# A two-layer hybrid attention and mixture-of-experts block: the sums of squares go behind the first sparse-query projection, the broadcast of their factors into the third

## The chip, the cores and the metric

The kernel runs on one core of a Trainium2 chip. The metric is the device time of one execution in microseconds (us), the median of several runs. The engines are TensorE (PE in the rows; its weight loads are PEld), VectorE (DVE), ScalarE (ACT), GpSimd (POOL) and SyncE (SP), whose queue issues nearly all DMA transfers. Each engine takes its instructions in the order in which the built program holds them.

## What is computed

512 tokens of width 1024 go through two layers. Each layer projects the tokens to many small groups of columns, runs two kinds of attention (a latent one with rotary keys and a sparse one that keeps 128 keys of each query), adds and normalises, and runs 16 experts, two per token. The part that matters here is this:

```python
proj = h @ w_in
qa, kva, kr, dq, dk, dv, iq, ik, iw = jnp.split(proj, SPLIT_POINTS, axis=-1)
# latent group (mla_group)
q = (rms_norm(qa, q_norm_g) @ w_q_up)      # qa has 384 columns
c_kv = rms_norm(kva, kv_norm_g)            # kva has 256 columns
k_nope, v = c_kv @ w_uk, c_kv @ w_uv
# rms_norm(x, g) = x * rsqrt(mean(x * x) + 1e-6) * g
# sparse group (dsa_group): queries dq (512 columns), keys dk, values dv;
# top_k over an index score made of iq, ik, iw selects the keys
```

## The kernel before

Everything is transposed: a projection's output has 128 columns of `w_in` on the partitions and the 512 tokens along the free axis. One such tile is made by `proj(ct)` (line 242): it splits 1024 columns of raw weights into a high and a low part (`granule`, line 170: ACT casts in line 163, and for tiles from the fourth on POOL subtracts in line 164) and multiplies, in `project` (line 266), high weights by high inputs, low weights by high inputs and high weights by low inputs, 8 matmuls each. So a projected tile costs 24 matmuls of 128x512 (line 271), of which the first 8 do without the low weights. The output lies in one of four PSUM buffers `mm`; two more are called `pv`.

The order of the tiles in a layer: S, two `iq`, `dkv`, then two `kva` among the index scores (lines 342 to 373), three `qa`, four `dq`. `qa` tiles are evacuated to `qg` by ACT (line 387) and DVE (line 388), and squared by ACT (line 389) into `sqq`; the third square lies in `sq2`, the second half of the tile `dkv` (the trace calls it dkv). The squares of `kva` are added into `sqk` (line 381). `dq` tiles are evacuated by ACT (line 405) and DVE (line 406) to a tile `dq`, one of nine buffers called `u4`, and copied to their places by DMA.

The norms' factors take this way. Sixteen matmuls with a column of ones (line 418) sum the squares over the partitions, into `pv`: four for `kva`, twelve for `qa`. DVE scales the sums (line 422, `ms`), POOL takes the power -0.5 (line 185, `rmsy`) and multiplies the identity by the factors (line 427, two instructions, the tile `dg`, called `dgt` in the code). Two matmuls of ones by `dg` (line 434) spread the factors over all partitions, one for the keys' side, one for the queries'. With the first, DVE scales `kvg` (line 439), ACT and POOL split it (`big<-kvg`), and PE makes the values v from it and the split weights `wv` (lines 220 to 223, four tiles `vs`). With the second, ACT and DVE make `ct` (lines 443, 444), by which DVE scales the latent queries (line 530, tile `q`). Then the heads begin: scores on PE (line 545), a minimum with the mask on DVE (line 490), exponential on ACT (line 492), scaling on DVE (line 498), transposes on PE (line 502).

All the while DVE has another job: the selection of 128 keys of each query, 16 rounds of MAX and MATCH_REPLACE (lines 365, 366) for each of three token blocks. A round's MATCH_REPLACE needs the MAX's result and the next MAX needs the MATCH_REPLACE's. These rounds have a lower priority (`LOWER`), so the scheduler fills DVE's queue with them between its other work.

A scheduler orders the instructions of each engine at build time, by priority (the order of the code) and by its own estimate of when an operand is there. `tc.issue_after(x)` makes what its block traces on the engine of `x` stand behind `x` there. Before the change the sums are written behind the second `dq` projection and the broadcast behind the third, with no such edge.

Of the kernel before, what the change touches and what calls it, by code (L numbers as in the profile page):

```python
# [17 lines left out]
L, T, D = 2, 512, 1024  # L18
NT = T // 128
# [18 lines left out]
T_S, T_IQ, T_DKV, T_KVA, T_QA, T_DQ = 0, 1, 3, 4, 6, 9  # L38
# [57 lines left out]
def block_kernel(ctx, tc, xT0, x0, win, wqk, wuv, wo, gvec, lnp, rw, rb, wgu, wdn, consts, angles, stripd, rowsd, out):  # L96
    nc = tc.nc
# [19 lines left out]
    def C(name, a=0, b=None):  # L117
        o, w = _C[name]
        return cn[:, o + a:o + (w if b is None else b)]
# [33 lines left out]
    def ps(tag):  # L153
        return psp.tile([128, 512], F32, name=tag, bufs={"mm": 4, "tr": 2, "pv": 2}[tag])
# [76 lines left out]
    def attention(l, xh, xl, wraw, first, rest, x_dram):  # L231
# [5 lines left out]
                    load_win(l, i, wraw)  # L237
            return wraw[s]

        done = {}  # L240

        def proj(ct):
            if l and ct == 0:

                raw((3 + AHEAD) // 2)
                for c in range(4):
                    done[c] = ps("mm" if c > 1 else "tr")
                for a in range(2):
                    if a:
                        rest()  # L250
                    for c in (0, 2):
                        order = (0, 1, 2) if a else (0, 2, 1)
                        for j in order:
                            for d in (c, c + 1):
                                project(done[d], first[d], slice(256 * a, 256 * (a + 1)), (j,), order[2])
            if ct not in done:
                done[ct] = ps("mm")
                project(done[ct], weights(ct), slice(0, T))
            return done.pop(ct)

        def weights(ct, eng=None):
            w = granule(raw(ct // 2), ct % 2, eng or (nc.gpsimd if ct >= 3 else None))
            if ct + AHEAD < N_COLT:
                raw((ct + AHEAD) // 2)
            return w

        def project(p, w, ts, jj=(0, 1, 2), end=2):
            for j in jj:
                for k in range(8):
                    x = (xl if j == 2 else xh)[k // 4][:, k % 4, ts]  # L270
                    nc.tensor.matmul(p[:, ts], w[j == 1][:, k * 128:(k + 1) * 128], x, start=(j + k == 0),  # L271
                                     stop=(j == end and k == 7))

        ke, ko = x4p("ke")
        at = u4("at")
# [10 lines left out]
        p = proj(T_S)  # L286
# [9 lines left out]
        for i in range(2):  # L296
            p = proj(T_IQ + i)
# [8 lines left out]
        p = proj(T_DKV)  # L306
# [7 lines left out]
        p = ps("mm")  # L314
# [6 lines left out]
        p = transpose4(dkv, 0)  # L321
        nc.scalar.copy(dvt, p.rearrange("p (a b) -> p a b", a=NT)[:, :, 64:128])
        p = transpose4(S, 0)
# [7 lines left out]
        sqk = u4p("sqk")  # L331
# [7 lines left out]
        for i in range(1, NT):  # L339
# [3 lines left out]
            for h in range(8):  # L343
                if (i, h) in KVA_AT:
                    latents(KVA_AT.index((i, h)))
                p = ps("mm")
                nc.tensor.matmul(p[:, :n], iq[h // 4][:, h % 4, (i - 1) * 128:i * 128], ik4[:, :n],
                                 start=True, stop=True)
# [4 lines left out]
                w = iwt[:, i, h:h + 1]  # L353
# [16 lines left out]
            for dd in DD[i]:  # L370
                w = dd.shape[1]
# [11 lines left out]
        sqq = list(u4p("sqq")) + [sq2]  # L383
        for i in range(3):
            p = proj(T_QA + i)
# [8 lines left out]
        for i in range(2):  # L394
            w = bigt()
# [4 lines left out]
        dqs = [bigt(F32R).rearrange("p (a b) -> p a b", a=4) for _ in range(2)]  # L400
        vs = bigt().rearrange("p (a b) -> p a b", a=4)
        for i in range(4):
            p = proj(T_DQ + i)
            qh, ql = u4p("dq", F32R)
            nc.scalar.activation(qh, p, AF.Copy, scale=-0.125)
            nc.vector.scalar_tensor_tensor(ql, p, -0.125, qh.bitcast(F32), op0=OP.mult, op1=OP.subtract)
            for s in range(2):
                d = dqs[i // 2][:, i % 2 * 2 + s, :]
                for j, q in enumerate((qh, ql)):
                    b = 64 * (s ^ j)  # L410
                    copy_rows(d[b:b + 64], q[64 * s:64 * (s + 1)])
            if i == 1:

                p = ps("pv")
                for j, qq in enumerate((sqk[:1], sqq)):
                    for t in range(NT):
                        for q in qq:
                            nc.tensor.matmul(p[:, j * 4 + t:j * 4 + t + 1], q[:, t * 128:(t + 1) * 128],
                                             C("ones", 0, 1), start=(q is qq[0]), stop=(q is qq[-1]))
                ms = sm.tile([128, 8], F32, name="ms")  # L420
                for j, n in enumerate((256, 384)):
                    nc.vector.tensor_scalar(ms[:, 4 * j:4 * j + 4], p[:, 4 * j:4 * j + 4], 1.0 / n, 1e-6,
                                            op0=OP.mult, op1=OP.add)
                rs, _ = rsqrt(ms, 8, "rms")
                dgt = u4("dg")
                for j in range(2):
                    nc.gpsimd.tensor_tensor(dgt[:, j * 512:(j + 1) * 512].rearrange("p (t a) -> p t a", t=NT),
                                            ident[:, None, :].to_broadcast([128, NT, 128]),
                                            rs[:, 4 * j:4 * j + 4][:, :, None].to_broadcast([128, NT, 128]), op=OP.mult)
            if i == 2:  # L430
                bc = []
                for j in range(2):
                    p = ps("pv")
                    nc.tensor.matmul(p, C("ones"), dgt[:, j * 512:(j + 1) * 512], start=True, stop=True)
                    bc.append(p)
        ckt = bigt(F32R)
        ckv = [(ckt[:, 1024 * i:1024 * i + 512], ckt[:, 1024 * i + 512:1024 * (i + 1)]) for i in range(2)]
        for i in range(2):
# [13 lines left out]
        for t in range(NT):  # L452
            p = ps("mm")
# [1033 lines left out]
```

## Time and profile before

| | us |
|---|---|
| median of 3 runs (lowest, highest) | 1191.95 (1191.82, 1192.46) |
| the profiled execution | 1192.57 |
| its span, first to last instruction | 1190.8 |
| PE busy with matmuls in the span | 1142.6 (96%) |
| DVE busy | 1020.2 (86%) |
| PE's weight loads busy | 893.5 (75%) |
| ACT busy | 791.2 (66%) |
| POOL busy | 285.6 (24%) |

The mean granted clock of TensorE is 0.986 of full speed. The first layer's attention lies at about 30 to 215 us of the span, the second layer's at about 620 to 805 us. Times in the rows are from the span's start. "128*128 128x512" is a matmul of a 128x128 stationary operand by 512 columns. A row of the timeline can merge several instructions (x24); its second number then runs from the first one's start to the last one's end. Text in brackets at a row's end is the idle time of the engine just before it and what ended that. A float32 matmul that is not marked for the faster format shows as two records, so the two broadcast matmuls are x4, and each sum is x2.

### The profile page before, as it was taken

What the parts mean: (1) busy time and instruction counts of PE and PEld (TensorE: products, weight loads), DVE (VectorE), ACT (ScalarE), POOL (GpSimd) and SP (SyncE); (2) the same over time, 40 slices, a digit from 0 to 9 for tenths busy, and PEclk for the clock granted to TensorE, in tenths of its full rate; (3) what the DMA queues carried; (4) which work ended last, traced back from release to release, by engine and by line L of the source; (5) the groups of instructions that cost most, each with busy time, mean ns of one, the idle gap of its engine ahead of it and who ended that gap; (6) DMA issues with size and microseconds to landing.
All of it is one profiled execution on the core that took longest, in us unless ns stands there. A gap on an engine that the chain in (4) does not pass through costs nothing. (4 is left out here: it accounts for less than half of the span.)

```text
span 1190.8 us, 16760 instructions
## 1 busy us (share of the span) xinstructions
PE 1142.6 (96%) x5705; PEld 893.5 (75%) x5705; DVE 1020.2 (86%) x1858; ACT 791.2 (66%) x1253; POOL 285.6 (24%) x236
## 2 busy tenths in 40 slices
PE   8999899999999999999998998999999999999996
PEld 6786555788788888887696765567887888888873
DVE  4599968399999999988957999774999999999898
ACT  4633668445888888887445346683468888888882
POOL 2345233121111111111132453422212111112011
PEclk9999999999999999999998999999999999999998
DMA  7626104366999999994735170144669999999841
GB/s 263 183 82 203 71 1 142 142 236 247 405 395 393 393 386 375 383 333 176 289 104 151 58 260 2 39 138 155 242 270 397 400 391 389 392 378 375 328 189 71
DMA packets 57547, 292.50 MB, mean 246 GB/s; under 512 B 10309, under 2 KB 14149, under 8 KB 29040
## 3 DMA queue, kind: packets, MB, share of 16 engines
q1 hardware_dynamic: 47664, 270.48, 60.9%
q0 software_dynamic: 8352, 15.66, 3.5%
q10 hardware_dynamic: 1440, 5.24, 1.1%
q8 instruction: 46, 0.75, 0.2%
q14 instruction: 45, 0.37, 0.1%
HBM read 267.96 MB, written 33.03 MB: 253 GB/s over the span
## 5 line engine op out<-in xcount | busy, mean ns | idle before, releaser
L163 ACT CAST hl<-big 128x1024 fp32r<-128x1024 f32 x438 | 457.4, 1054 | 123.0 <-PE mm L1065 51.3
L164 DVE TENSOR_TENSOR hl<-big,hl 128x1024 fp32r<-128x1024 f32 x403 | 483.7, 1227 | 47.7 <-ACT hl L163 41.7
L1064 PE MATMUL mm<-hl,xh 128*128 128x512 f32 x504 | 207.2, 411 | 0.6 <-ACT hl L163 0.6
L1065 PE MATMUL mm<-hl,xh 128*128 128x512 f32 x504 | 197.3, 392 | 0.0
L1086 PE MATMUL pv<-hl,hT 128*128 128x512 f32 x720 | 169.9, 390 | 0.1
L1086 PEld LDWEIGHTS pv<-hl,hT 128*128 128x128 f32 x720 | 134.7, 188 | 28.7 <-DVE hl L164 1.0
L271 PE MATMUL mm<-big,hl 128*128 128x512 f32 (+1 forms) x624 | 140.3, 384 | 2.4 <-ACT big L163 1.7
L271 PEld LDWEIGHTS mm<-big,hl 128*128 128x128 f32 x624 | 112.9, 193 | 27.7 <-ACT hl L163 2.3
L164 POOL TENSOR_TENSOR hl<-big,hl 128x1024 fp32r<-128x1024 f32 x35 | 86.5, 2476 | 133.7 <-ACT hl L163 118.2
L1028 POOL DMA_INDIRECT xg<-xdr,ii x30 | 54.0, 1800 | 268.9 <-DVE ii L1042 242.4
L1064 PEld LDWEIGHTS mm<-hl,xh 128*128 128x128 f32 x504 | 94.8, 188 | 16.8 <-ACT hl L163 1.1
L1065 PEld LDWEIGHTS mm<-hl,xh 128*128 128x128 f32 x504 | 95.1, 189 | 15.7
L1065 PE MATMUL mm<-hl,xl 128*128 128x512 f32 x252 | 98.9, 392 | 0.0
L1064 PE MATMUL mm<-hl,xl 128*128 128x512 f32 x252 | 98.8, 392 | 0.0
L635 PE MATMUL mm<-hl,big 128*128 128x512 f32 x384 | 93.4, 396 | 0.0
L492 ACT ACTIVATE P<-P,mn 128x128 f32<-128x128 f32 (+3 forms) x128 | 71.9, 569 | 17.2 <-DVE mn L490 14.8
L635 PEld LDWEIGHTS mm<-hl,big 128*128 128x128 f32 x384 | 70.8, 188 | 13.6
L1106 POOL DMA_INDIRECT ydr<-y,ii x28 | 30.2, 1079 | 189.4 <-ACT y L1102 117.5
L504 ACT COPY big<-tr 128x512 f32<-128x512 f32 (+3 forms) x128 | 49.8, 432 | 36.5 <-PE tr L502 35.6
L502 PE MATMUL tr<-cn,P 128*128 128x128 f32 x320 | 61.9, 293 | 9.1 <-DVE P L498 8.3
L502 PEld LDWEIGHTS tr<-cn,P 128*128 128x128 f32 x320 | 36.2, 141 | 41.7 <-ACT big L504 17.1
L572 POOL TENSOR_TENSOR mh<-dd,cn 128x256 f32<-128x256 f32 (+2 forms) x64 | 44.6, 718 | 64.9 <-DVE mn L490 39.5
(277 smaller groups left out, 1816.7 us busy)
## 6 DMA issues: line engine op xcount, KB each, us to landing
big<-wgu SPq DMA_DIRECT2D x128, 1024.0 KB, 8.2
big<-wdn SPq DMA_DIRECT2D x64, 1024.0 KB, 7.9
big<-win SPq DMA_DIRECT2D x10, 1024.0 KB, 5.4
ydr<-zz SPq DMA_DIRECT2D x2, 4096.0 KB
big<-wo SPq DMA_DIRECT2D x8, 1024.0 KB, 14.8
big<-ydr SPq DMA_DIRECT2D x8, 1024.0 KB, 12.7
big<-wqk SPq DMA_DIRECT2D x4, 1024.0 KB, 5.1
big<-dq SPq DMA_DIRECT2D x32, 128.0 KB, 2.3
```

Of the source, the lines that this page charges most:

```text
L163: i = nc.scalar.copy(hi, src).ins
L164: last_lo[0] = (eng or nc.vector).tensor_sub(lo, src, hi.bitcast(F32)).ins
L271: nc.tensor.matmul(p[:, ts], w[j == 1][:, k * 128:(k + 1) * 128], x, start=(j + k == 0), stop=(j == end and k == 7))
L492: nc.scalar.activation(e, e, AF.Exp, bias=mn[:, i:i + 1], scale=-1.0, accum_out=su[:, i:i + 1])
L502: nc.tensor.transpose(p[:, (i - kb) * 128:(i - kb + 1) * 128], P[:, PO[i] + kb * 128:PO[i] + (kb + 1) * 128], ident)
L504: copies.append(nc.scalar.copy(pt[kb], p[:, :512 - 128 * kb]).ins)
L572: last_mask[0] = nc.gpsimd.tensor_tensor(m[:, c:c + w], dd, C("slope", h, h + 1).to_broadcast([128, w]), op=OP.mult)
L635: R["pe"] = nc.tensor.matmul(pp[t][i], x, w[:, i * 512:(i + 1) * 512], start=first, stop=last).ins
L1028: return nc.gpsimd.indirect_dma_start(out=st[e]["xg"], out_offset=None, in_=xdr[l], in_offset=bass.IndirectOffsetOnAxis(ap=st[e]["ii"][:, ...
L1064: nc.tensor.matmul(pg, x, w[:, :512], start=(k == 0 and x is a and w is wh), stop=last)
L1065: nc.tensor.matmul(pu, x, w[:, 512:], start=(k == 0 and x is a and w is wh), stop=last)
L1086: nc.tensor.matmul(py[i], x, w[:, i * 512:(i + 1) * 512], start=(k == 0 and x is a and w is wh), stop=last)
```

## The change

Two steps move. The sums of squares and what follows them (`ms`, `rmsy`, `dg`) are written behind the first of the four `dq` projections, not the second, and an edge keeps the sums behind that projection's last matmul on PE. The broadcast is put inside the third `dq` projection: behind its first 8 matmuls (the ones with high weights), ahead of its other 16, with edges on both sides. `project` notes its last matmul for this. No instruction is added or removed in the source.

```diff
-        done = {}
+        done, last_mm = {}, [None]
...
-                    nc.tensor.matmul(p[:, ts], w[j == 1][:, k * 128:(k + 1) * 128], x, start=(j + k == 0),
-                                     stop=(j == end and k == 7))
+                    last_mm[0] = nc.tensor.matmul(p[:, ts], w[j == 1][:, k * 128:(k + 1) * 128], x,
+                                                  start=(j + k == 0), stop=(j == end and k == 7)).ins
...
         for i in range(4):
-            p = proj(T_DQ + i)
+            if i != 2:
+                p = proj(T_DQ + i)
+            else:
+
+                p, w, bc = ps("mm"), weights(T_DQ + i), []
+                project(p, w, slice(0, T), (0,))
+                with tc.issue_after(last_mm[0]):
+                    for j in range(2):
+                        bc.append(ps("pv"))
+                        b = nc.tensor.matmul(bc[j], C("ones"), dgt[:, j * 512:(j + 1) * 512], start=True, stop=True)
+                with tc.issue_after(b.ins):
+                    project(p, w, slice(0, T), (1, 2))
...
-            if i == 1:
+            if i == 0:
 
                 p = ps("pv")
-                for j, qq in enumerate((sqk[:1], sqq)):
-                    for t in range(NT):
-                        for q in qq:
-                            nc.tensor.matmul(p[:, j * 4 + t:j * 4 + t + 1], q[:, t * 128:(t + 1) * 128],
-                                             C("ones", 0, 1), start=(q is qq[0]), stop=(q is qq[-1]))
+                with tc.issue_after(last_mm[0]):
+                    for j, qq in enumerate((sqk[:1], sqq)):
+                        for t in range(NT):
+                            for q in qq:
+                                nc.tensor.matmul(p[:, j * 4 + t:j * 4 + t + 1], q[:, t * 128:(t + 1) * 128],
+                                                 C("ones", 0, 1), start=(q is qq[0]), stop=(q is qq[-1]))
...
-            if i == 2:
-                bc = []
-                for j in range(2):
-                    p = ps("pv")
-                    nc.tensor.matmul(p, C("ones"), dgt[:, j * 512:(j + 1) * 512], start=True, stop=True)
-                    bc.append(p)
```

In the changed kernel the lines of the sums, the broadcast, ACT's and DVE's evacuation of dq, `ms`, `dg` and the scaling of `kvg` are 430, 412, 416, 417, 434, 439 and 445; from there on each line number is 6 higher than before.

The built order moves in the same way in both layers; the excerpts are from the first. On PE, before, from the `qa` and `dq` projections on (120 matmuls are three `qa` and two `dq` tiles):

```order
L271 MATMUL mm<-big,hl 128x512 x120
L418 MATMUL pv<-cn,sqq 128x1 x2
L418 MATMUL pv<-cn,dkv 128x1
L418 MATMUL pv<-cn,sqq 128x1 x2
L418 MATMUL pv<-cn,dkv 128x1
L418 MATMUL pv<-cn,sqq 128x1 x2
L418 MATMUL pv<-cn,dkv 128x1
L418 MATMUL pv<-cn,sqq 128x1 x2
L418 MATMUL pv<-cn,dkv 128x1
L271 MATMUL mm<-big,hl 128x512 x24
L434 MATMUL pv<-dg,cn 128x512 x2
L271 MATMUL mm<-big,hl 128x512 x24
```

On PE, now, the same place (96 matmuls are three `qa` tiles and one `dq` tile; behind the broadcast 40 matmuls follow, 16 of the third and 24 of the fourth `dq` tile):

```order
L271 MATMUL mm<-big,hl 128x512 x96
L430 MATMUL pv<-cn,sqk 128x1 x4
L430 MATMUL pv<-cn,sqq 128x1 x2
L430 MATMUL pv<-cn,dkv 128x1
L430 MATMUL pv<-cn,sqq 128x1 x2
L430 MATMUL pv<-cn,dkv 128x1
L430 MATMUL pv<-cn,sqq 128x1 x2
L430 MATMUL pv<-cn,dkv 128x1
L430 MATMUL pv<-cn,sqq 128x1 x2
L430 MATMUL pv<-cn,dkv 128x1
L271 MATMUL mm<-big,hl 128x512 x32
L412 MATMUL pv<-dg,cn 128x512 x2
```

All sixteen sums now stand behind the first `dq` tile; before, the scheduler had put the four of `sqk` ahead of the `qa` tiles, among the index scores. Between sums and broadcast there are now 32 projection matmuls, where there were 24.

On POOL, before (hl_890 is the low part of the fourth `dq` tile's weights, hl_939 that of `wv`, hl_974 and hl_985 those of the next weights):

```order
L164 TENSOR_TENSOR hl_890<-big_686,hl_890 128x1024
L164 TENSOR_TENSOR hl_939<-wv_746,hl_939 128x1024
L185 TENSOR_TENSOR rmsy_845<-ms_842,mhalf_81 128x8
L427 TENSOR_TENSOR dg_847<-cn_75,rmsy_845 128x512 x2
L164 TENSOR_TENSOR hl_974<-big_748,hl_974 128x1024
L164 TENSOR_TENSOR hl_985<-big_748,hl_985 128x1024
```

On POOL, now:

```order
L164 TENSOR_TENSOR hl_890<-big_686,hl_890 128x1024
L185 TENSOR_TENSOR rmsy_810<-ms_807,mhalf_81 128x8
L439 TENSOR_TENSOR dg_812<-cn_75,rmsy_810 128x512 x2
L164 TENSOR_TENSOR hl_939<-wv_746,hl_939 128x1024
L164 TENSOR_TENSOR hl_974<-big_748,hl_974 128x1024
L164 TENSOR_TENSOR hl_985<-big_748,hl_985 128x1024
```

The power and the two products with the identity have moved ahead of the split of `wv`.

On ACT, before, with the semaphores that each instruction waits for (the first `dq` tile is dq_783; it takes the buffer in which `wv` lay, so it waits for POOL's split of `wv`):

```order
L389 ACTIVATE dkv_299<-mm_715 128x512 [waits DVE_49]
L163 CAST hl_939<-wv_746 128x1024 [waits DMAHW7_49,PE_49,Pool_49]
L405 ACTIVATE dq_783<-mm_755 128x512 [waits Pool_49]
L163 CAST hl_974<-big_748 128x1024 [waits DMAHW5_49,PE_49]
L405 ACTIVATE dq_818<-mm_790 128x512 [waits PE_49]
```

On ACT, now (dq_783 takes the buffer of `sqq`, free when PE has made the sums; it is the second tile, dq_843, that takes the buffer of `wv`):

```order
L389 ACTIVATE dkv_299<-mm_715 128x512 [waits DVE_49]
L416 ACTIVATE dq_783<-mm_755 128x512 [waits PE_49,Activation_49]
L163 CAST hl_939<-wv_746 128x1024 [waits DMAHW7_49,Pool_49]
L416 ACTIVATE dq_843<-mm_815 128x512 [waits PE_49,Pool_49]
L163 CAST hl_974<-big_748 128x1024 [waits DMAHW5_49]
```

The wait for POOL's split of `wv` has passed from the first `dq` tile to the second. On DVE, now, from `ms` on to the second `dq` tile (before, `ms` stood four rounds later and behind the first `dq` tile, and the second `dq` tile one round behind `ms`):

```order
L434 TENSOR_SCALAR ms<-pv 128x4 x2
L366 MATCH_REPLACE aw<-m_493,aw 128x384
L417 SCALAR_TENSOR_TENSOR dq<-mm,dq 128x512
L365 MAX m_496<-aw 128x8
L366 MATCH_REPLACE aw<-m_496,aw 128x384
L365 MAX m_499<-aw 128x8
L366 MATCH_REPLACE aw<-m_499,aw 128x384
L365 MAX m_502<-aw 128x8
L366 MATCH_REPLACE aw<-m_502,aw 128x384
L365 MAX m_505<-aw 128x8
L366 MATCH_REPLACE aw<-m_505,aw 128x384
L417 SCALAR_TENSOR_TENSOR dq<-mm,dq 128x512
```

and DVE, before, the same step:

```order
L406 SCALAR_TENSOR_TENSOR dq<-mm,dq 128x512
L366 MATCH_REPLACE aw<-m_499,aw 128x384
L365 MAX m_502<-aw 128x8
L366 MATCH_REPLACE aw<-m_502,aw 128x384
L365 MAX m_505<-aw 128x8
L422 TENSOR_SCALAR ms<-pv 128x4 x2
L366 MATCH_REPLACE aw<-m_505,aw 128x384
L365 MAX m_508<-aw 128x8
L406 SCALAR_TENSOR_TENSOR dq<-mm,dq 128x512
```

So `ms` stands at the MAX of m_493 now, and between it and the second `dq` tile lie the rest of that round, the first `dq` tile and four whole rounds. From the second `ct` on, DVE's order is as before. SP's order is the same in both kernels.

## Rows read from the trace of the kernel before

**Rows 1.** Busy time by stretch, both layers; columns: engines' busy us, granted clock, DMA.

```profile
core 0: us, PE busy (x) PEld busy (x) DVE busy (x) ACT busy (x) POOL busy (x), PEclk, DMA share, GB/s
43.00:134.00 91.00, 85.98 (x368) 64.93 (x369) 87.75 (x218) 40.99 (x85) 34.97 (x20) 0.96 0.41 138
633.60:724.60 91.00, 85.38 (x368) 64.85 (x368) 87.65 (x217) 40.80 (x84) 32.40 (x19) 0.96 0.39 132
```

**Rows 2.** Timeline of PE, layer 1; columns: start, us, engine, line, operation, operands, idle.

```profile
59.62 24.57 PE L271 MATMUL mm<-big,hl 128*128 128x512 f32 x107
84.03 0.50 PE L418 MATMUL pv<-cn,sqq 128*128 128x1 f32 x4
...
86.63 5.75 PE L271 MATMUL mm<-big,hl 128*128 128x512 f32 x24
94.17 3.00 PE L434 MATMUL pv<-dg,cn 128*128 128x512 f32 x4 [1.80 <-POOL dg L427]
96.19 7.21 PE L271 MATMUL mm<-big,hl 128*128 128x512 f32 x24
103.24 0.39 PE L220 MATMUL mm<-hl,big 128*128 128x512 f32 x1
```

**Rows 3.** Timeline of PE, layer 2.

```profile
684.80 2.12 PE L434 MATMUL pv<-dg,cn 128*128 128x512 f32 x4 [1.79 <-POOL dg L427]
...
692.25 0.39 PE L220 MATMUL mm<-hl,big 128*128 128x512 f32 x1
...
705.98 3.11 PE L545 MATMUL mm<-ke,q 128*128 128x384 f32 x4 [1.00 <-DVE q L530]
```

**Rows 4.** Timeline of DVE, layer 1.

```profile
85.11 0.56 DVE L365 MAX8 m<-aw 128x8 f32<-128x384 f32 x1
...
87.61 0.56 DVE L365 MAX8 m<-aw 128x8 f32<-128x384 f32 x1
88.09 0.67 DVE L406 SCALAR_TENSOR_TENSOR dq<-mm,dq 128x512 fp32r<-128x512 f32 x1
...
89.32 0.56 DVE L365 MAX8 m<-aw 128x8 f32<-128x384 f32 x1
...
91.05 0.21 DVE L422 TENSOR_SCALAR ms<-pv 128x4 f32<-128x4 f32 x2
...
116.59 0.28 DVE L490 CUSTOM_DVE_ANT_0 P<-mm,at 128x128 f32<-128x128 f32 x1
```

**Rows 5.** Timeline of DVE, layer 2: the same first minimum.

```profile
707.23 0.28 DVE L490 CUSTOM_DVE_ANT_0 P<-mm,at 128x128 f32<-128x128 f32 x1
```

**Rows 6.** Timeline of ACT, layer 1.

```profile
80.83 0.60 ACT L389 ACTIVATE dkv<-mm 128x512 f32<-128x512 f32 x1 [0.26 <-DVE qg L388]
...
85.42 0.60 ACT L405 ACTIVATE dq<-mm 128x512 fp32r<-128x512 f32 x1 [3.06 <-POOL hl L164]
```

**Rows 7.** Timeline of POOL, layer 1.

```profile
91.34 1.66 POOL L185 TENSOR_TENSOR rmsy<-ms,mhalf 128x8 f32<-128x8 f32 x1 [5.96 <-DVE ms L422]
...
95.07 4.71 POOL L164 TENSOR_TENSOR hl<-big,hl 128x1024 fp32r<-128x1024 f32 x2
```

**Rows 8.** Busy time in the three stretches in which the granted clock was 0.50.

```profile
95.30:98.70 3.40, 3.40 (x7) 1.98 (x8) 3.26 (x9) 0.00 (x0) 3.40 (x2) 0.50 0.51 119
149.90:153.30 3.40, 3.05 (x10) 2.10 (x12) 3.40 (x15) 1.98 (x7) 1.37 (x3) 0.50 0.00 0
706.30:709.70 3.40, 3.40 (x6) 1.68 (x5) 3.37 (x13) 1.70 (x6) 0.00 (x0) 0.50 1.02 329
```

**Rows 9.** Timeline of DVE later in the heads, layer 1, then the same instructions, layer 2.

```profile
136.22 0.43 DVE L164 TENSOR_TENSOR big<-pv,big 128x256 fp32r<-128x256 f32 x1 [1.45 <-ACT big L163]
...
158.56 0.29 DVE L490 CUSTOM_DVE_ANT_0 P<-mm,at 128x128 f32<-128x128 f32 x1 [2.02 <-PE mm L545]
...
727.35 0.43 DVE L164 TENSOR_TENSOR big<-pv,big 128x256 fp32r<-128x256 f32 x1 [1.57 <-ACT big L163]
...
748.57 0.29 DVE L490 CUSTOM_DVE_ANT_0 P<-mm,at 128x128 f32<-128x128 f32 x1 [1.31 <-PE mm L545]
```

## The prediction, written before the changed kernel ran

> **What bounds the kernel now.** I read the busy time by stretch first. From the start of the index selection to the first softmax DVE is busy 87.75 of 91 us in layer 1 and 87.65 in layer 2, PE with matmuls 85.98 and 85.38 [rows 1]; the rest of DVE's time is the small step between instructions, and the list of waits has no DVE entry in either stretch. So two engines are nearly full, and busy time alone doesn't say which sets the pace.
>
> The timeline of PE shows what the change aims at: PE reaches the broadcast and idles 1.80 us in layer 1 and 1.79 in layer 2 until POOL has `dg` [rows 2, 3]. In layer 1 the granted clock is then 0.50 (the 1.2 GHz level) from 95.3 to 98.7 [rows 8], and the fourth `dq` tile takes 7.21 us, the third 5.75 [rows 2].
>
> Whether that wait costs anything can be read by laying the layers side by side, since only one of them had the slow clock there. The broadcasts start at 94.17 and 684.80, 590.63 apart. The values' first matmul starts at 103.24 and 692.25, 589.01 apart: layer 2's PE has gained 1.62 us [rows 2, 3]. The first minimum on DVE starts at 116.59 and 707.23, 590.64 apart [rows 4, 5]: **the gain is gone to 0.01 us**. A little before it, layer 2's PE stood still for DVE's latent queries, 1.00 us in one place [rows 3]. So in this stretch DVE sets the pace, and time that PE saves ends as a longer wait for DVE.
>
> **The change part by part.** I follow layer 1; layer 2 has the same order and durations. Each step starts from the trace's own time and adds durations.
>
> *The sums.* 107 matmuls take 24.41 us up to the sums (59.62 to 84.03), 0.228 each, a tile 5.47. The first `dq` tile ends one tile ahead of the old sums, at 78.56. Twelve sums take 2.60 us (84.03 to 86.63), 0.217 each; the four of `sqk` that now join them 0.87 [rows 2]. But the third square is not there: ACT makes it from 80.83 to 81.43, because it stands behind DVE's evacuation of the third `qa` tile [rows 6]. PE, whose queue holds the sums ahead of the second `dq` tile, gets through `sqk` and two more sums by about 79.9 and **waits some 1.5 us until 81.43**. Ten sums remain, 2.2 us: they end at 83.7.
>
> *The factors.* DVE takes `ms` at the MAX that starts at 85.11; its slot opens 0.48 later, as `dq`'s does at 87.61, so at 85.59 [rows 4]. The sums are there; no wait. From `ms` to the broadcast's first `dg` the trace has 3.12 us (91.05 to 94.17) [rows 2, 4]; `dg` is there at 88.7, its second half a microsecond on.
>
> *The broadcast.* PE runs the second `dq` tile from 83.7 to 89.2 and 8 matmuls of the third (1.82) to 91.0. `dg` is there: the wait of 1.80 is gone. The broadcast takes 2.02 at most (94.17 to 96.19, partly at the slow clock), then 40 matmuls 9.1: the values start at 102.1. In layer 1 that is 1.1 us earlier than 103.24, in layer 2 0.5 later than 101.62 (692.25 less 590.63). PE has traded one wait for another, and the sums of `sqk`, which stood in a stretch where PE waited for ACT, now stand in its full stretch.
>
> *POOL's queue and what it holds up.* This is the term that I think reaches the end. The power and both products now stand ahead of the split of `wv`. In the trace the split behind them starts 4.02 us behind `ms` (91.05 to 95.07) and takes 2.36 (half of 4.71) [rows 4, 7]. From 85.59 that gives an end at 91.97. The buffer of `wv` is what the second `dq` tile is written to; in the kernel before the first `dq` tile had it, and ACT stood 3.06 us for that same split [rows 6]. So ACT writes the second `dq` tile from 92.0 to 92.6, though PE has had it since 89.2. DVE's part stands behind it in DVE's strict order. DVE gets there at 91.7: from 85.11 one round with a `dq` in it (1.71, as 87.61 to 89.32), three plain rounds (1.25, half of 85.11 to 87.61) to 90.57, and about 1.15 of a fourth [rows 4]. **DVE waits 0.9 us**, and it had no wait in this stretch. What else moves on DVE keeps its count; a `dq` costs 0.46 there whichever gap of a round it fills (1.71 less 1.25), and the scaling of `kvg`, which no longer stands next to a `dq`, fills one gap more, which I estimate at 0.1 gained. Net +0.8 us on DVE per layer.
>
> *What is late next.* POOL splits `kvg` behind the next two weights, and the second of these waits for the third `dq` tile, on PE at 96.7; with ACT's and POOL's steps as in [rows 6, 7] its end comes at about 102.7, when PE wants it. PE's fourth `v` tile waits for a buffer that DVE frees with the last `dq`; PE then comes to the first scores no later than before in layer 1, and at most half a microsecond later in layer 2, where it waited 1.00 for DVE. Neither moves DVE. SP's order is unchanged, and its copies of `dq` move by less than a transfer's slack to the first sparse head.
>
> *Does a DVE delay last to the end?* A delay that the slow clock gave layer 2 at its first scores is still 0.49 at 727.35, against layer 1 (591.13 - 590.64) [rows 4, 5, 9], and up to there DVE has no idle time to give back until the 1.45 us ahead of 136.22, which is the end of a chain that itself starts at DVE.
>
> **Sum.** Two layers by 0.8: +1.6 to +1.7 us. On the profiled execution's 1192.57 that is 1194.2; the runs' median lies 0.62 below that execution, so I expect 1193.6. The unknown is how much of 0.8 arrives. Its bounds: nothing (the later idle on DVE takes it up), 1.8 (two layers by 0.9).
>
> **Rivals.**
>
> *Nothing arrives* (1192.0). The 1.45 us ahead of 136.22 [rows 9] would have to be slack of its own and swallow 0.8. Against it: it ends a chain through DVE's own softmax.
>
> *PE sets the pace after all* (1189). If DVE's rounds could slide, the lost idle time of 1.80 and 1.79, and the slow clock's 1.62, would all count: at most -5.2, of which the new wait of 1.5 per layer takes 3.0 back, so -2.2; with a shorter new wait, because the third square comes earlier, -3. The alignment to 0.01 us speaks against it. The Trainium skill's page "Perfetto Trace Analysis", section "Optimization Strategies", says that the matmul engine should be kept as busy as possible and that what it waits for is to be optimised. By that rule this change takes away the right wait; the rows of DVE say otherwise here, where the two layers show what such a wait was worth.
>
> *Slower by the clock* (1195.0). PE now idles 1.5 us behind the first `dq` tile, and DVE's 0.8 is added to PE's waits at the first scores. In the trace the granted clock was 0.50 three times [rows 8]. Where it hits the projections, DVE doesn't notice. Where it hits the heads, DVE waits for PE: from the minimum of 116.59 to 136.22 the layers part by 0.49 (706.3 to 709.7 was in layer 2), and from 136.22 to 158.56 they come together by 1.12 (591.13 to 590.01), which is layer 1's stretch of 149.9 to 153.3 [rows 4, 5, 8, 9]. One more such stretch in the heads costs 0.5 to 1.1; from the first scores on it counts. With one added, 1193.6 + 1.1 and a little: about 1195. For it: more idle time on PE just ahead of the heads. Against it: the old idle time of 1.80 is gone, and the stretch at 95.3 with it.
>
> *The broadcast still waits*, so that the change doesn't do what it says: `dg` at 88.7 against 91.0 leaves 2.3 us; I give it nothing of its own.
>
> **How the numbers follow.** Forecast 1193.6: 0.52. Nothing arrives, 1192.0: 0.17. PE sets the pace, 1189: 0.10. Slower by the clock, 1195.0: 0.21. A measurement can tell about 0.2%, 2.4 us: below 1189.6 is faster, above 1194.3 slower. Most of the third rival is faster, 0.07; the last one and the upper edge of the forecast (a stall of 0.9 kept whole, and a stretch of slow clock half counted) are slower, 0.27; the same 0.66. The range from 1191.2 to 1195.4 leaves out PE's rival and the last one with two such stretches.
>
> **What would show it.** Right: DVE idle about 0.9 us ahead of its second `dq` (line 417), released by ACT, in both layers; PE idle 1.5 us at the sums (line 430), released by ACT, and none at line 412; DVE's first minimum about 0.8 later from its selection's start than before (116.59), while the values on PE start earlier in layer 1. Wrong: DVE without that idle time, which would mean POOL or the buffer was quicker than I read; or DVE's first minimum earlier than before, which would mean that PE set the pace.

## The result, and the profile after

The changed kernel takes 1199.72 us, the median of five runs (1197.81 to 1200.04). Five runs of the kernel before, beside them, gave 1191.95 us (1190.41 to 1194.26). The ratio is 1.0053, 95% interval 1.0042 to 1.0064: **slower by 6.3 us**, outside the range of 1191.2 to 1195.4. This ratio is not the quotient of the two medians, which is 1.0065 or 7.8 us; the text goes by the ratio throughout. The profiled execution took 1200.04 us, its span 1198.3 (before: 1192.57 and 1190.8).

The timeline of PE in the changed kernel, the place of [rows 2], answers first: the sums (line 430), the second tile and a third of the third (line 271 x32), the broadcast (line 412) and the values' first matmul (line 220). The first four rows are of layer 1, the next three of layer 2.

```profile
81.54 0.38 PE L430 MATMUL pv<-cn,dkv 128*128 128x1 f32 x2 [1.98 <-ACT dkv L389]
...
85.44 9.12 PE L271 MATMUL mm<-big,hl 128*128 128x512 f32 x32
94.40 1.88 PE L412 MATMUL pv<-dg,cn 128*128 128x512 f32 x4
...
105.23 0.39 PE L220 MATMUL mm<-hl,big 128*128 128x512 f32 x1
...
675.58 0.38 PE L430 MATMUL pv<-cn,dkv 128*128 128x1 f32 x2 [1.85 <-ACT dkv L389]
...
679.58 9.01 PE L271 MATMUL mm<-big,hl 128*128 128x512 f32 x32
688.42 1.88 PE L412 MATMUL pv<-dg,cn 128*128 128x512 f32 x4
```

The wait of 1.80 us at the broadcast is gone: line 412 has no bracket. In its place PE waits 1.98 and 1.85 us for the third square. Then 32 matmuls take 9.12 us where 24 took 5.75 before [rows 2]. The reason stands in the busy time by stretch (columns as in [rows 1]; the granted clock is the third figure from the end): half clock, the 1.2 GHz level, for 6.8 us behind the wait, in both layers, and two more stretches in the heads.

```profile
43.00:134.00 91.00, 85.52 (x357) 65.81 (x358) 86.23 (x210) 37.50 (x75) 34.73 (x20) 0.94 0.42 138
...
82.00:88.80 6.80, 6.80 (x26) 6.12 (x26) 6.51 (x19) 1.54 (x2) 3.85 (x4) 0.50 0.18 41
675.90:682.70 6.80, 6.80 (x26) 6.13 (x26) 6.53 (x19) 1.54 (x2) 3.76 (x3) 0.50 0.18 46
153.70:157.10 3.40, 3.40 (x12) 2.02 (x12) 3.40 (x12) 2.64 (x9) 1.36 (x3) 0.50 0.00 0
747.60:751.00 3.40, 3.40 (x12) 2.06 (x14) 3.40 (x14) 2.40 (x9) 1.36 (x3) 0.50 0.00 0
```

DVE is the engine that the prediction followed. Its timeline in layer 1, and the POOL rows of the same microseconds:

```profile
93.47 0.69 DVE L417 SCALAR_TENSOR_TENSOR dq<-mm,dq 128x512 fp32r<-128x512 f32 x1 [1.61 <-ACT dq L416]
...
104.11 1.57 DVE L368 TENSOR_TENSOR aw<-aw 128x384 f32<-128x384 f32 x1
105.60 0.68 DVE L365 MAX8 m<-aw 128x8 f32<-128x512 f32 x1
106.20 1.04 DVE L372 SCALAR_TENSOR_TENSOR dd<-aw,at 128x384 f32<-128x384 f32 x1
```

```profile
89.67 2.41 POOL L164 TENSOR_TENSOR hl<-wv,hl 128x1024 fp32r<-128x1024 f32 x1
...
101.60 2.41 POOL L164 TENSOR_TENSOR hl<-big,hl 128x1024 fp32r<-128x1024 f32 x1 [4.77 <-ACT hl L163]
103.97 2.86 POOL L164 TENSOR_TENSOR big<-kvg,big 128x512 fp32r<-128x512 f32 x2
```

Two losses stand there. DVE waits 1.61 us at its second `dq` (1.51 in layer 2), the place that was predicted, with 0.9. And the last two instructions of the third block's selection, the comparison (line 368) and the distances (line 372), take 1.57 and 1.04 us. Before they took 0.55 and 0.54, and POOL's split of `kvg` was over at 102.3, ahead of them. Now the two meet. The rows before:

```profile
102.45 0.55 DVE L368 TENSOR_TENSOR aw<-aw 128x384 f32<-128x384 f32 x1
...
103.52 0.54 DVE L372 SCALAR_TENSOR_TENSOR dd<-aw,at 128x384 f32<-128x384 f32 x1
```

```profile
99.77 2.55 POOL L164 TENSOR_TENSOR big<-kvg,big 128x512 fp32r<-128x512 f32 x2
102.38 0.95 POOL L448 MEMSET zz<- 128x1024 f32 x1
```

POOL's memset, which reads no tile, ran beside the comparison there and cost it nothing. MAX8 (line 365), which stands between the two in the changed kernel beside the same split, takes its usual 0.68. Layer 2 has the same pair, 1.57 and 1.04 us.

Laid side by side instruction by instruction, DVE is 0.06 us later than before until 85, 1.67 later behind the wait, 3.2 later behind the two long instructions, and stays near there to the end of the layer (3.5); layer 2 adds another 3.1, and its heads 0.9. That makes the 7.5 us by which the two profiled spans differ. Per layer: 1.6 of waiting and 1.5 of collision, (1.57 + 1.04) - (0.55 + 0.54). Twice that is 6.2, beside 6.3 by the ratio.

### The profile page after: what moved, and what is told of

Read it like the earlier page. It is cut to its first block, busy times and chain, and to the rows that moved or that the text cites. A ratio compares the mean times of both kernels' runs of the same rounds, so it can differ in the third digit from the quotient of the medians.

```text
span 1198.3 us, 16756 instructions
## 1 busy us (share of the span) xinstructions
PE 1149.7 (96%) x5705; PEld 898.4 (75%) x5705; DVE 1022.8 (85%) x1858; ACT 790.7 (66%) x1253; POOL 285.5 (24%) x236
```

## Experiments

Each ran beside the kernel before on the same chip; a difference in us is its ratio less one, on about 1193.

### The sums alone

```diff
-            if i != 2:
-                p = proj(T_DQ + i)
-            else:
...
+            p = proj(T_DQ + i)
...
+            if i == 2:
+                bc = []
...
+                    nc.tensor.matmul(p, C("ones"), dgt[:, j * 512:(j + 1) * 512], start=True, stop=True)
```

> Only the sums are moved: they stand behind the first tile of the third projection, as in the changed kernel; the broadcast stands behind the third tile, as in the kernel before. Theory (the loss comes with the sums: PE waits 1.98 us for the third square, works at a granted clock of 0.50 afterwards, so the second tile comes late and DVE waits 1.6 us, and the POOL split of kvg then lies beside DVE's L368 and L372, 1.5 us): all three are still there, the time is that of the changed kernel, 1198.5 to 1200.5. Rival (the broadcast inside the tile is what costs): the time is that of the kernel before, 1191 to 1193.

Measured 1197.07 us, ratio 1.0024 (1.0015 to 1.0034): +2.9 us, between theory and rival. DVE's rows:

```profile
94.17 0.69 DVE L406 SCALAR_TENSOR_TENSOR dq<-mm,dq 128x512 fp32r<-128x512 f32 x1 [1.47 <-ACT dq L405]
...
104.94 0.94 DVE L368 TENSOR_TENSOR aw<-aw 128x384 f32<-128x384 f32 x1
106.41 0.53 DVE L372 SCALAR_TENSOR_TENSOR dd<-aw,at 128x384 f32<-128x384 f32 x1
```

The wait is whole, the collision only touches (0.38 us a layer). So the sums bring the wait; the broadcast's new place moves POOL and DVE against each other by the rest.

### The sums eight matmuls later

Inside the second tile, behind its first eight matmuls, where the third square is there:

```diff
-            if i == 0:
+            elif i == 1:
+                p, w = ps("mm"), weights(T_DQ + i)
+                project(p, w, slice(0, T), (0,))
...
+                with tc.issue_after(bz.ins):
+                    project(p, w, slice(0, T), (1, 2))
```

> The changed kernel with the sums eight matmuls later, inside the second tile, where the third square (ready at 81.4 us in the first layer) is there already. Theory (PE's wait for the square starts the loss): no wait of PE at the sums, granted clock 1.00 through the second tile, no wait of DVE of over 0.3 us at the second tile's remainder, the kvg split on POOL back at about 99 to 102 us and L368 and L372 at 0.55 and 0.54 us; time 1191 to 1193. Rival (what costs is that the factors come early, so that POOL does rms and dg ahead of the split of wv): DVE still waits about 0.9 us, time 1193.5 to 1196. Second rival (the broadcast's two matmuls inside the third tile put PE behind for the heads): 1197 or more with no wait of DVE before 100 us.

Measured 1198.21 us, 1.0037 (1.0027 to 1.0048): +4.4 us. The theory's PE part came true: no wait at the sums and a clock of 1.00 from there to 110 us (PE waits 1.12 us ahead of the eight matmuls instead, and 1.00 at the broadcast). Its time did not. The rows of ACT, DVE and POOL in turn:

```profile
94.85 0.60 ACT L438 ACTIVATE dq<-mm 128x512 fp32r<-128x512 f32 x1 [4.99 <-POOL hl L164]
```

```profile
95.48 0.69 DVE L439 SCALAR_TENSOR_TENSOR dq<-mm,dq 128x512 fp32r<-128x512 f32 x1 [0.91 <-ACT dq L438]
...
104.41 0.55 DVE L368 TENSOR_TENSOR aw<-aw 128x384 f32<-128x384 f32 x1
105.47 2.22 DVE L372 SCALAR_TENSOR_TENSOR dd<-aw,at 128x384 f32<-128x384 f32 x1
```

```profile
92.44 2.38 POOL L164 TENSOR_TENSOR hl<-wv,hl 128x1024 fp32r<-128x1024 f32 x1
...
104.88 2.40 POOL L164 TENSOR_TENSOR hl<-big,hl 128x1024 fp32r<-128x1024 f32 x1
```

With PE out of the way the wait is 0.91 us, released through ACT by POOL's split of `wv`: the prediction's own term, in place and size. And another split of POOL now meets the distances, which take 2.22.

### The second tile in a buffer of its own

```diff
-            qh, ql = u4p("dq", F32R)
+            qh, ql = (h2("dq", F32R), h2("dq", F32R)) if i == 1 else u4p("dq", F32R)
```

> The changed kernel with the second tile of dq in a buffer of its own, so that its copy on ACT no longer needs the buffer that POOL's split of wv frees at 92.08 us; every queue has the same order. Theory (in the changed kernel DVE's wait of 1.6 us is set by PE, whose second tile is ready only at 92.8 us after the stretch at a granted clock of 0.50): the wait stays at 1.5 to 1.7 us in each layer and the time at 1198 to 1200.5. Rival (the step of the prediction: POOL's split of wv sets the wait): the wait falls under 0.3 us and the time to 1196 to 1197.5.

Measured 1196.37 us, 1.0031 (1.0018 to 1.0044): +3.7 us, and the row decides for PE:

```profile
92.79 0.60 ACT L416 ACTIVATE dq<-mm 128x512 fp32r<-128x512 f32 x1 [6.42 <-PE mm L271]
```

```profile
93.42 0.69 DVE L417 SCALAR_TENSOR_TENSOR dq<-mm,dq 128x512 fp32r<-128x512 f32 x1 [1.54 <-ACT dq L416]
...
104.06 0.55 DVE L368 TENSOR_TENSOR aw<-aw 128x384 f32<-128x384 f32 x1
105.13 1.05 DVE L372 SCALAR_TENSOR_TENSOR dd<-aw,at 128x384 f32<-128x384 f32 x1
```

The buffer is free and DVE waits 1.54 us, nearly as long as in the changed kernel (2.71 in layer 2, where the half clock lasted longer, and 0.28 at `ms`). So two causes end within a microsecond of each other, PE's tile at 92.8 and POOL's split at 92.1; taking one away shows the other. In this run the comparison escaped: it starts at 104.06 and goes through, and POOL's `kvg` split of 104.03 takes 3.29 us instead of 2.55. But the longer wait of layer 2 takes most of that back (5.6 against 6.2 in the table below), so why the time is 1.6 us below the expected isn't shown.

### The comparison and the distances later

```diff
+                if i == 3 and k == 3:
+                    with tc.issue_after(mr):
+                        distances(2, *held)
...
+            if i == 2:
+                held = work, acc
+            else:
+                distances(i, work, acc)
```

> The changed kernel with DVE's two instructions of two SBUF operands on the third block (the comparison that ends its selection and the distances, L368 and L372, 1.57 and 1.04 us in the changed kernel) moved behind the fourth round of the fourth block's selection, to about 111 to 113 us of the first layer, past POOL's split of kvg (103.97 to 106.83 us). Nothing else moves in any queue. Theory (they are slow because POOL's split runs beside them): 0.55 and 0.54 us there, or one of the two still longer if the next split of POOL (about 112 us) reaches it; 1.0 to 1.5 us less in each layer, time 1196.5 to 1198. DVE's wait of 1.6 us at the second tile stays. Rival (they are slow by what they wait for, or PE sets the pace there): the same time as the changed kernel, 1199 to 1200.5.

Measured 1196.17 us, 1.0028 (1.0018 to 1.0038): +3.3 us, where the changed kernel has +6.3. As the theory has it:

```profile
111.49 0.54 DVE L374 TENSOR_TENSOR aw<-aw 128x384 f32<-128x384 f32 x1
112.56 0.53 DVE L378 SCALAR_TENSOR_TENSOR dd<-aw,at 128x384 f32<-128x384 f32 x1
```

With the waits of 1.58 and 1.60 us left, 3.2 is what remains, and 3.3 is measured.

### All three taken away

The sums later, the buffer, and the distances behind the third round (`k == 2`), together.

> The changed kernel with all three causes taken away: the sums eight matmuls later (no wait of PE for the third square), the second tile of dq in a buffer of its own (no wait for POOL's split of wv), and DVE's L368 and L372 behind the third round of the fourth block's selection, at about 108 to 111 us, where POOL is idle. Theory (these three are the whole loss, and DVE sets the pace, so that PE's gain is worth nothing): no wait of DVE over 0.3 us between 80 and 112 us, L368 and L372 at 0.55 and 0.54 us, and the time of the kernel before within 1 us, 1192 to 1194. Rival (PE's freed 1.8 us a layer do reach the end once nothing else is lost): 1189 to 1191. Second rival (something else of the change costs time as well): 1195 or more.

Measured 1192.14 us beside 1192.63, 0.9996 (0.9987 to 1.0005): **the loss is gone, and nothing is gained.** DVE's rows show no wait over 0.3 us between 80 and 112 us and 0.56 and 0.54 for the pair. PE's rows at the broadcast and the first scores show what becomes of its lead in layer 1 (1.3 us at 98 us, once DVE's starts ahead of the change are set equal):

```profile
91.36 2.12 PE L445 MATMUL pv<-dg,cn 128*128 128x512 f32 x4 [0.99 <-POOL dg L433]
...
114.60 0.92 PE L565 MATMUL mm<-ke,q 128*128 128x128 f32 x4 [0.67 <-ACT ke L556]
116.22 1.77 PE L565 MATMUL mm<-ke,q 128*128 128x384 f32 x4 [0.70 <-DVE q L550]
122.75 0.33 PE L522 MATMUL tr<-cn,P 128*128 128x128 f32 x1 [1.03 <-DVE P L518]
```

The wait of 0.67 us for ACT stands in the kernel before too. For DVE PE waits 0.70 and 1.03 us, where it waited 0.63 in the kernel before: 1.1 of the 1.3 us end there. The run tests less than its expectation says. PE still waits about 1 us at the broadcast in both layers, and in layer 2 it comes to the values no earlier than before (693.40 and 692.25 us, with DVE's start 1.1 us later in this profile). So only layer 1 gave PE a lead, and the rival, which counted on 1.8 us a layer, was not tried in full.

### POOL beside DVE in the kernel before

```diff
         zz = u4("zz")
+        for i in range(2):
+            nc.gpsimd.tensor_sub(zz[:, 512 * i:512 * (i + 1)], kvg[0], kvg[1])
```

> The kernel before with two idle subtractions of 128x512 on POOL (their result is overwritten by the memset of zz) right behind the split of kvg, so that POOL works beside DVE's L368 (102.45 us) and L372 (103.52 us) as it does in the changed kernel; DVE, PE and ACT have the same order as before. Theory (the collision alone costs 1.5 us a layer, and DVE sets the pace): L368 and L372 take about 1.5 and 1.0 us, time 1194 to 1195.5. Rival (DVE has slack behind this point, or POOL's work does not slow it): 1191.5 to 1192.5.

The rows are as the theory has them, without any other part of the change:

```profile
103.53 1.54 DVE L368 TENSOR_TENSOR aw<-aw 128x384 f32<-128x384 f32 x1
105.60 1.03 DVE L372 SCALAR_TENSOR_TENSOR dd<-aw,at 128x384 f32<-128x384 f32 x1
```

```profile
103.35 2.87 POOL L448 TENSOR_TENSOR zz<-kvg 128x512 f32<-128x512 f32 x2
```

The time is not: 1194.12 us lies in the expected range, but the kernel before took 1193.41 beside it; the ratio is 1.0003 (0.9994 to 1.0012), +0.4 where two collisions of 1.5 make 3.0. In its trace DVE is 1.5 us later behind the pair and 0.65 later at 158 us; of layer 2's 1.5, 1.25 remain. The same with one long subtraction instead of two short ones:

```diff
+        nc.gpsimd.tensor_sub(zz, kvt, kvt)
```

> The kernel before with one idle subtraction of 128x1024 on POOL (about 2.4 us) behind the split of kvg, in place of the two of 128x512 (about 1.3 us each) of the earlier run; the same bytes, and every other queue as in the kernel before. Theory (DVE's instruction with two SBUF operands makes no progress until POOL's running instruction ends): L368, which starts with it at about 102.5 us, takes 2.4 to 2.8 us instead of 1.5, and L372, which then comes behind it, 0.55. Rival (the two share what they need and both go slower): L368 1.0 to 1.6 us and L372 about 1.0 us, as with the two short ones. Time in either case 1193 to 1196.

```profile
103.15 2.13 DVE L369 TENSOR_TENSOR aw<-aw 128x384 f32<-128x384 f32 x1
...
105.81 0.53 DVE L373 SCALAR_TENSOR_TENSOR dd<-aw,at 128x384 f32<-128x384 f32 x1
```

```profile
102.97 1.90 POOL L448 TENSOR_TENSOR zz<-kvg 128x1024 f32<-128x1024 f32 x1
```

One long POOL instruction, one long DVE instruction, and the next one free: DVE's comparison ends 0.41 us behind POOL's end (105.28 and 104.87), a little less than its own 0.55. So the two don't share in this row: DVE stands until POOL's instruction is over. Time 1195.20, 1.0012 (1.0003 to 1.0022), +1.4 for 3.2 on DVE. Where the rest of such a delay goes in the kernel before stays open: its own profile has a stretch of half clock in the heads at 149.9 us [rows 8] that neither of these two profiles has, which may be much of it.

### PE kept busy through its wait

Sixteen small matmuls whose result isn't used stand ahead of the sums (`warm`), and the second tile has a buffer of its own as above:

```diff
-                with tc.issue_after(last_mm[0]):
+                with tc.issue_after(warm(8, p, last_mm[0])):
                     for j, qq in enumerate((sqk[:1], sqq)):
```

> The changed kernel with the second tile of dq in a buffer of its own and 16 small matmuls of 256 columns, whose result is not used, put ahead of the sums, so that PE works through the 2 us in which it waits for the third square. Theory (the idle time at the sums is what the granted clock of 0.50 follows): clock 1.00 through sums and second tile, the sums in 2.5 us or less instead of 3.7, the second tile ready at 89 to 90 us instead of 92.8. Rival (the low clock has another origin): 0.50 there all the same, and the second tile at 92 to 93 us. The queue of DVE has another order here, so the whole time decides nothing.

One execution, 1200.63 us. By stretch:

```profile
78.00:85.00 7.00, 6.57 (x54) 6.10 (x54) 6.72 (x17) 4.31 (x7) 2.36 (x1) 1.00 0.28 77
85.10:88.50 3.40, 3.40 (x9) 2.67 (x8) 3.26 (x11) 0.50 (x1) 0.55 (x1) 0.50 0.17 39
```

Theory and rival are each right in part: the sums behind the wait, 0.43 us now, run at full clock (81.63 to 83.89, 2.3 us against 3.9), but the clock still falls, later and for half as long, and ACT has the second tile at 91.28 (92.84 in the changed kernel). In layer 2, where PE still waited 1.69 us, the clock fell for 6.8 us.

### Less work on DVE, and the changed kernel again

Three runs leave out one round of selection, of the fourth block (the third with `i == 2`):

```diff
-            for _ in range(16):
+            for _ in range(16 - (i == 3)):
```

> The kernel before with 15 rounds of selection instead of 16 for the fourth block (it keeps 120 keys there instead of 128), which takes one MAX8, one load and one MATCH_REPLACE8 of 512 columns, 0.69, 0.09 and 0.68 us, off DVE in each layer and nothing off PE. Theory (DVE sets the pace from the selection to the end of the heads' first part): 1.4 us less in each layer, 1189.5 to 1191.5. Rival (PE sets the pace): no difference, 1192.5 to 1194.

Measured 1193.67 us, 1.0008 (1.0000 to 1.0017): no gain. The round is taken off the end of the fourth block's selection, at about 141 us, and there DVE now waits for PE:

```profile
142.42 0.69 DVE L530 TENSOR_TENSOR q<-mm,ct 128x512 f32<-128x512 f32 x1 [0.78 <-PE mm L223]
144.48 0.69 DVE L530 TENSOR_TENSOR q<-mm,ct 128x512 f32<-128x512 f32 x1 [0.76 <-PE mm L223]
```

That is the rival's outcome: PE holds DVE up as soon as DVE has a round less here, so DVE alone does not set the pace to the end of the selection. How far it does, this run doesn't say.

> The kernel of the run with all three causes taken away, with 15 rounds of selection instead of 16 for the third block (it keeps 120 keys there instead of 128): 0.56, 0.09 and 0.54 us less on DVE in each layer, ahead of the first scores. The queue of DVE is planned anew behind it. Theory (PE comes early to the first scores there and waits for DVE's queries, 0.67 and 0.70 us at 114.6 and 116.2 us, so DVE's time counts in full): 1.2 us less in each layer than without, 1189 to 1191 where the kernel before takes 1192 to 1193.5. Rival (behind the first scores PE sets the pace): 1191.5 to 1193.5.

> The same round less for the third block in the kernel before, 1.2 us less on DVE in each layer. Theory (in the kernel before PE comes to the first scores only 0.67 us ahead of DVE's queries, 114.95 us, so no more than that can be gained): 0 to 0.7 us less in each layer, 1191 to 1193. Rival (DVE alone sets the pace in the kernel before too): 2.4 us less, 1189.5 to 1191.

Both became slower, +4.5 us (1.0038, 1.0025 to 1.0051) and +2.4 us (1.0020, 1.0011 to 1.0029), and decide nothing on the pace. A shorter queue was planned anew, and the new order brought collisions: the comparison took 1.00 and in layer 2 2.58 us, the distances 1.43, in the first; 0.81 and 0.98 in the second.

> The changed kernel again, unaltered, beside the kernel before on one chip, so that it stands on the same footing as the other runs. Theory (two waits of DVE of 1.6 us and two collisions of 1.5 us, 6.2 us in all): 1198 to 1200 where the kernel before takes 1192 to 1193.5. Rival (part of the first difference came from stretches at half clock that only some executions have): 1196.5 to 1198.

Measured 1200.35 us, just above the expected, 1.0059 (1.0046 to 1.0073): +7.0 us, with waits of 1.59 and 1.63 and the same 1.57 and 1.04 in both layers. The sum from DVE's rows is 6.3.

The sums of DVE's waits and of the pair's excess over 0.55 + 0.54, both layers, against the times:

| kernel | waits | pair | sum | measured (95%) |
|---|---|---|---|---|
| changed | 3.1 | 3.0 | 6.2 | 6.3 (5.0 to 7.6) |
| changed, again | 3.2 | 3.0 | 6.3 | 7.0 (5.5 to 8.7) |
| sums later | 1.8 | 3.4 | 5.2 | 4.4 (3.2 to 5.7) |
| own buffer | 4.5 | 1.0 | 5.6 | 3.7 (2.1 to 5.2) |
| sums alone | 3.1 | 0.8 | 3.8 | 2.9 (1.8 to 4.1) |
| distances later | 3.2 | 0.0 | 3.2 | 3.3 (2.1 to 4.5) |
| all three | 0.0 | 0.0 | 0.0 | -0.5 (-1.6 to 0.6) |
| before, two short | 0.0 | 3.0 | 3.0 | 0.4 (-0.7 to 1.4) |
| before, one long | 0.0 | 3.2 | 3.2 | 1.4 (0.4 to 2.6) |

Each sum is of one profiled execution, each time of all of them. Six of the nine sums lie in their intervals; those of the own buffer and of the kernel before with POOL's extra work lie above. One reason shows in the traces. In these three, in the sums alone, the sums later, the distances later and the changed kernel again, DVE's delay shrinks by 1.1 us between 135 and 157 us of layer 1, where the profile of the kernel before has its half clock [rows 8] and theirs have none. How many executions of the kernel before have that stretch isn't known.

## Why the prediction was wrong, step by step

- **That DVE sets the pace, so that PE's wait was worth nothing**: right as far as it was tested. The wait at the broadcast went, and no time came of it; with the three losses taken away the time is that of before, and the lead that PE then had in layer 1 ended as waits for DVE. It does not hold to the end of the selection: with a round less, DVE waits for PE at 142 us.
- **PE waits 1.5 us at the sums**: right in place, 1.98 and 1.85 in size; PE came there earlier than reckoned.
- **The second tile from 83.7 to 89.2**: the first step that failed. The rows that it was made from have full clock. The changed kernel has half clock from 82.0 to 88.8; ten sums took 3.9 us instead of 2.2, and ACT had the tile at 92.84. The prediction said of a half clock in the projections that "DVE doesn't notice"; with the sums in front of the tile it does. So the values on PE, which were to start earlier in layer 1, start at 105.23, 2.0 us later than before [rows 2].
- **POOL holds the second tile, DVE waits 0.9**: the mechanism is there (split of `wv` over at 92.08, predicted 91.97; 0.91 us with PE's lateness gone), but in the changed kernel PE ends later than POOL. So the sign that was named, DVE idle at line 417 and released by ACT, came in the right place with another cause behind it, which is chance. The term is 1.6, not 0.8 a layer: 1.5 of the 4.6 us by which the sum was short.
- **What is late next: the split of `kvg`, "when PE wants it", "neither moves DVE"**: failed, and it is the larger part, 3.0 us. The split's end was put at 102.7; it came at 106.8, and from its start at 103.97 it runs beside DVE's comparison. I asked only who waits for the split, not what runs beside it. The Trainium skill has the rule, on the page "SBUF — State Buffer", section "SBUF: two separate sides": VectorE with two SBUF inputs and a GpSimd instruction that reads SBUF share one pair of ports under an exclusive lock, held for a whole instruction, and the loser blocks. The rows agree (2.13 us beside one long instruction, 1.54 and 1.03 beside two short ones). Such a meeting could have been read from the kernel before, as the rows under this list show.
- **A delay of DVE lasts to the end**: it did here (table, first rows); for a collision alone in the kernel before less than half was measured.
- **Slower by the clock**: the rival's stretches in the heads did come in the profile, two of them, and DVE's delay grows there by 0.3 to 0.9 us; it is not what makes the 6 us.

The kernel before has such meetings of its own. Where DVE adds up the index scores (line 358, two SBUF operands), one instruction takes 0.60 us alone and 2.76 and 2.74 beside POOL's splits, and ends 0.4 us behind each split:

```profile
64.40 2.76 DVE L358 SCALAR_TENSOR_TENSOR aw<-big,iwt,aw 128x384 f32<-128x384 f32 x1
...
67.74 0.60 DVE L358 SCALAR_TENSOR_TENSOR aw<-big,iwt,aw 128x384 f32<-128x384 f32 x1
...
70.13 2.74 DVE L358 SCALAR_TENSOR_TENSOR aw<-big,iwt,aw 128x384 f32<-128x384 f32 x1
```

```profile
64.02 2.72 POOL L164 TENSOR_TENSOR hl<-big,hl 128x1024 fp32r<-128x1024 f32 x1 [2.60 <-ACT hl L163]
69.46 3.00 POOL L164 TENSOR_TENSOR hl<-big,hl 128x1024 fp32r<-128x1024 f32 x1 [2.72 <-ACT hl L163]
```

Layer 2 has 2.75 us twice (655.03 and 660.75). A timeline over the whole stretch merges fourteen of these instructions into one row, and the two long ones don't stand out. So some 4.3 of the 87.75 us that the prediction read as DVE at work [rows 1] are DVE standing still for POOL. What it would give to part these two was not tried.

## What to carry to other kernels

When an edit moves work on POOL, write down which VectorE instructions with two SBUF operands now run beside it: in these traces the meeting cost the rest of POOL's instruction, no wait showed it, and only the instruction's own duration gave it away. Look for it one instruction at a time, since merged rows hide it. Two operands aren't the only case: four scalings of the heads that read one tile (line 498) take 3.63 us beside POOL at 146.56 in the kernel before, and 1.27 with POOL idle at 121.54. Where two engines hold up the same tile, price both; the one that you took from rows at full clock may be the later. And freeing an engine that then waits for another gained nothing here: PE's lead of 1.3 us ended as waits for DVE.

## What the runs showed of the hardware

A wait of 1.3 to 2.0 us between matmuls of one column was followed by half clock in all five traces that have it in both layers (the changed kernel twice, the sums alone, the own buffer, the distances later), for 6.8 us in layer 1 each time and 6.8 or 10.2 in layer 2. The kernel before waited 1.80 and 1.79 us ahead of the broadcast, and its clock fell in layer 1 alone [rows 2, 3, 8]. With a wait of 1.1 us ahead of eight full matmuls and then the same sums it was not settled: full clock in two traces (the sums later, all three taken away), 6.8 us at half clock in layer 1 of the third (all three, one round less):

```profile
80.00:85.00 5.00, 4.80 (x35) 4.45 (x35) 4.79 (x13) 2.86 (x5) 2.36 (x1) 1.00 0.13 17
85.00:91.80 6.80, 6.80 (x21) 5.64 (x21) 6.52 (x20) 1.64 (x2) 2.19 (x2) 0.50 0.27 91
```

Executions of one kernel differ in their mean clock, and in their time with it. The twelve of the kernel with the sums later fall into two groups, 1195.6 to 1197.6 us at a mean granted clock of 0.987 or 0.988 and 1198.9 to 1199.9 at 0.981 or 0.982: about 3 us, half of what the change itself made. Its one trace is of the faster group, and its median of 1198.21 lies between the two; which stretches the slower group has more, no trace shows.
